# Seven products of 2x2 block sums for 6 of 16 row blocks in both MLPs, weights in groups of three blocks

## The chip, the cores and the metric

The kernel runs on one core of one Trainium2 chip. The metric is device time in microseconds of one execution; the median of 3 runs of the kernel before is 2336.47 us (2336.16 to 2338.05). The engines of the core are named as the profile names them: PE (TensorE, matrix products), PEld (its weight loads), DVE (VectorE), ACT (ScalarE), POOL (GpSimd), SP (SyncE, which issues the loads of the weights).

## The reference, cut to what matters

A two-layer encoder for 256 tokens of width 2048, all in float32: a sparse-attention mixer in layer 0, a convolution module in layer 1, and behind each of them an MLP of hidden width 8192 and a gated embedding. The change is in the two MLPs.

```python
D_MODEL, SEQ, D_FF = 2048, 256, 8192

def sq_relu_mlp(hn, w1, w2):
    a = jax.nn.relu(hn @ w1)
    return (a * a) @ w2

def reference(...):
    h = x
    for i in range(2):
        hn = rmsnorm(h, norm_mix_g[i])
        h = h + (dsa_mixer(hn, ...) if i == 0 else conformer_conv(hn, ...))
        h = h + sq_relu_mlp(rmsnorm(h, norm_mlp_g[i]), mlp_w1[i], mlp_w2[i])
        h = h + jax.nn.sigmoid(h @ ple_w_gate[i]) * (p[i] @ ple_w_proj[i])
    return rmsnorm(h, final_g)
```

## The kernel before, in words

Every large product is `gemm(x, src)` (L205): 256 tokens (two tiles `t` of 128) by 2048 rows of weights (16 row blocks `k` of 128) by 512 columns. The two token tiles accumulate in two PSUM banks `pm[0]`, `pm[1]`. For float32 accuracy each operand is a pair of parts of 12 significant bits, high and low, and one block product is three matmuls (L189 to L191): high by high, high by low, low by high. The activations stand as pairs `xh`, `xl` (128 features on the partitions, 16 blocks, 256 tokens). The weights are loaded by SP as they are, four row blocks to a transfer of 1 MB (`KG` = 4, tile `raw`, 4 buffers), and split in the kernel two blocks at a time: ACT copies `raw` to the high part `wh` (L181), DVE subtracts to get the low part `wl` (L185); 5 buffers each. PE then does 12 matmuls with these two blocks: 2 blocks, 2 token tiles, 3 parts.

An MLP (L568) goes over its hidden width in four parts of 2048 (`blk`). In a part, four gemms with columns of `w1` give the hidden values; `act` applies relu and the norm's factor (ACT, L579), squares (DVE, L580), and one step later PE transposes (L587, 4 of 128x128 for each token tile) and `split` (L212, ACT L215 and DVE L216) makes the pair `a`. Then four gemms with rows of `w2` follow, and DVE adds their banks to the residual stream `h` (`add_h`, L276). An MLP is so 32 gemms of 96 matmuls, and both together 64.

Work that belongs to a finished product (evictions, transposes) is put off into the following product by `defer` and `step` (L100, L103): a step is made for every two row blocks. The order on each engine is set by a scheduler that takes the recorded instructions with a priority by their place in the program and its own estimate of when their operands and buffers are ready. The profile's times are the chip's, not this estimate's. Each engine then works through its own list in order; a waiting instruction holds up all behind it.

In the convolution module some of the subtractions run on POOL. The first products of the kernel wait for the first transfers; the last gemm (L627) does the products of token tile 1 from the 6th row block on last, so that the end of tile 0 lies beside them.

Of the kernel before, what the change touches and what calls it, by code (L numbers as in the profile page):

```python
# [23 lines left out]
KG = 4  # L24
# [27 lines left out]
POOL_FROM = 1  # L52


@with_exitstack
def encoder(ctx: ExitStack, tc: tile.TileContext, A, inv_freq, out):
# [31 lines left out]
    def work(*shape):  # L88
        """A tile of up to 512 words per partition, from one rotation."""
        return shaped(small.tile([P, NB], F32, name="work", tag="work", bufs=6), shape)  # L90

    def held(*shape):
        """The same, from the rotation of tiles that live longer."""
        return shaped(small.tile([P, NB], F32, name="held", tag="held", bufs=5), shape)

# [61 lines left out]

    def blocks(w, n0, n=NB):
        return w.rearrange("(k p) n -> p k n", p=P)[:, :, n0:n0 + n]

    def gemm_part(pm, x, src, k0, kn, kt, low=None, dma=KG, apart=99):
# [3 lines left out]
        raw, rest = None, []  # L165
        for j in range(0, kn, 2):
            step()
            k = k0 + j
            if j % dma == 0:
                d = min(dma, kn - j)  # L170
                raw = wpool.tile([P, KG, NB], F32, name="raw", tag="raw", bufs=4)[:, :d, :n]
                if len(src.shape) == 3:
                    nc.sync.dma_start(raw, src[:, k:k + d])
                else:
                    m = src.shape[3]
                    for s in range(src.shape[2]):
                        nc.sync.dma_start(raw[:, :, s * m:(s + 1) * m], src[:, k:k + d, s])
            r = raw[:, j % dma:j % dma + 2, :]
            wh = wpool.tile([P, 2, NB], F32R, name="wh", tag="wh", bufs=5)[:, :, :n]
            wl = wpool.tile([P, 2, NB], F32R, name="wl", tag="wl", bufs=5)[:, :, :n]  # L180
            recent[0] = nc.scalar.activation(wh, r, AF.Copy).ins  # L181
            eng = low or nc.vector
            if callable(eng):
                eng = eng(k)
            eng.tensor_tensor(wl, r, wh.bitcast(F32), op=ALU.subtract)  # L185
# [7 lines left out]
            if j >= apart:  # L193
                for i in range(2):
                    products(i, 0)
                    rest.append(lambda i=i, products=products: products(i, 1))
            else:
                order = [(i, t) for i in range(2) for t in range(TT)]
                if k + 2 == kt:
                    order.sort(key=lambda v: v[1])  # L200
                for i, t in order:
                    products(i, t)
        return rest

    def gemm(x, src, low=None, tiles=mm_tile, dma=KG):  # L205
        step()
        pm = [tiles() for _ in range(TT)]
        kt = src.shape[1]
        gemm_part(pm, x, src, 0, kt, kt, low, dma)
# [11 lines left out]
    def rpow(dst, src, eps, scale=1.0):  # L221
        """dst = (scale * src + eps) ** -0.5"""
# [5 lines left out]
    class Norm:  # L228
        """Sums of squares of h by chunk, and in the end 1 / rms of every token."""
# [23 lines left out]

    def h_half(kk, x, g):
# [4 lines left out]
        if g is None:  # L259
            split(x[0][:, kk:kk + 2, :], x[1][:, kk:kk + 2, :], pt.rearrange("p k t f -> p k (t f)"))  # L260
        else:
            for k in range(2):
                split(x[0][:, kk + k, :], x[1][:, kk + k, :], pt[:, k].rearrange("p t f -> p (t f)"),
                      g[:, kk + k:kk + k + 1])
# [18 lines left out]
    def embedding(i):  # L283
        """The per-layer embedding, transposed and split."""
# [5 lines left out]
        ph = small.tile([P, 2, S], F32R, name="ph", bufs=1)  # L290
        pl = small.tile([P, 2, S], F32R, name="pl", bufs=1)
# [25 lines left out]
    # =================== layer 0: sparse attention ===================  # L317
    with tc.tile_pool(name="att", bufs=1) as att:
# [16 lines left out]
        def angles():  # L335
            """cos and sin of the rotary angles"""
# [24 lines left out]
        def rope(v, t, nh, rot):  # L361
            """v [P, nh, 128]: rotate the first `rot` of each head, in place"""
# [11 lines left out]
        def heads(pm, rot, dst):  # L374
            """[tokens, heads x 128] in PSUM -> scaled, rotated, transposed to dst [P, heads, S]"""
# [16 lines left out]
        norm0 = norm  # L392
        vv = att.tile([P, TT, NB], F32, name="vv")
        pm = gemm(xA, blocks(w_in, V0), dma=2)
# [153 lines left out]
        pms = []  # L548
        for c in range(2):
            step()  # L550
            pms.append([mm_tile() for _ in range(TT)])
            gemm_part(pms[c], xB, w_out[:, :, c * NB:(c + 1) * NB], 0, KT - KG, KT)
        flush()

    xA = xpair("A")
    norm = Norm()
    for c in range(4):
        w = w_out[:, :, c * NB:(c + 1) * NB]
        if c < 2:
            pm = pms[c]  # L560
            gemm_part(pm, xB, w, KT - KG, KG, KT)
        else:
            pm = gemm(xB, w)
        defer(0, lambda c=c, pm=pm: add_h(c, pm))
        h_chunk(c, xA, gcol["mlp0"], norm)

    # =================== squared-ReLU MLP ===================
    def mlp(layer, x, norm, other, xname):  # L568
        w1, w2 = A["mlp_w1"][layer], A["mlp_w2"][layer]
        xn = None  # L570
        for blk in range(4):
            a = xpair(other)

            def act(c, pm, a):
                rs = []
                for t in range(TT):
                    r = held(4, P)
                    rf = r.rearrange("p k f -> p (k f)")
                    nc.scalar.activation(rf, pm[t], AF.Relu, scale=norm[t])  # L579
                    nc.vector.tensor_tensor(rf, rf, rf, op=ALU.mult)  # L580
                    rs.append(r)

                def turn():
                    for t in range(TT):
                        pt = tr_tile().rearrange("p (k f) -> p k f", k=4)
                        for k in range(4):
                            nc.tensor.transpose(pt[:, k, :], rs[t][:, k, :], ident)  # L587
                        sl = (slice(None), slice(4 * c, 4 * c + 4), slice(t * P, (t + 1) * P))
                        split(a[0][sl], a[1][sl], pt)
                defer(1, turn)  # L590

            for c in range(4):
# [4 lines left out]
            for c in range(4):  # L597
                pm = gemm(a, blocks(w2[blk * D:(blk + 1) * D], c * NB))
                defer(0, lambda c=c, pm=pm: add_h(c, pm))
                if blk == 3:  # L600
                    h_chunk(c, xn)
        return xn

    # =================== gated per-layer embedding ===================
# [59 lines left out]
    xA = mlp(0, xA, norm, "B", "A")  # L664
# [5 lines left out]
    # =================== layer 1: convolution module ===================  # L670
    with tc.tile_pool(name="cnv", bufs=1) as cnv:
# [31 lines left out]
        def conv_pe(kk):  # L703
            """Depthwise convolution as products with diagonal matrices."""
# [18 lines left out]
        def conv_dve(tiles):  # L723
            """Depthwise convolution of one or two tiles, in two independent chains of sums."""
# [114 lines left out]
        xB = xpair("B")  # L839
        norm = Norm()  # L840
        for c in range(4):
            bb = cnv.tile([P, NB], F32, name="bb", tag="bb", bufs=2)
# [9 lines left out]
    xB = mlp(1, xB, norm, "A", "B")  # L852
# [55 lines left out]
```

## Time and profile before

| | us |
|---|---|
| median of 3 runs | 2336.47 |
| span of the profiled execution, first to last instruction | 2334.4 |
| PE busy | 2317.6 |
| PEld busy | 1928.5 |
| DVE busy | 1381.5 |
| ACT busy | 1109.4 |
| POOL busy | 243.0 |

The span is that of the profiled execution; the time of that execution around its span is not shown, so that the difference to the median, 2.07 us, stands for what lies outside. "Busy" adds up the recorded intervals of an engine, overlaps counted once. For PE they are modelled ends of pipelined matmuls: two matmuls that follow each other overlap in the record, and the distance of their starts says what one takes of PE's time.

### The profile page before, as it was taken

To read this page: it belongs to the slowest core of one execution; us is meant where nothing else is said; L and a number is where in the kernel's file an instruction comes from. 1 tells how busy PE (TensorE), PEld (TensorE's weight loads), DVE (VectorE), ACT (ScalarE), POOL (GpSimd) and SP (SyncE) were. 2 spreads that over 40 slices of the span, in tenths; PEclk is the share of its full clock that TensorE was granted. 3 is DMA by queue.
4 is the path that set the end of the run, shared out by engine and by line. 5 is a ranking of instruction groups with operands and counts; after the bars stand their busy time and mean duration, and the time that the engine had idled before them with its cause. 6 is when DMAs were issued, how large, how long until landed. Compare 5 with 4: busy or idle time off the path is not lost.

```text
span 2334.4 us, 27458 instructions
## 1 busy us (share of the span) xinstructions
PE 2317.6 (99%) x10798; PEld 1928.5 (83%) x10798; DVE 1381.5 (59%) x1796; ACT 1109.4 (48%) x1424; POOL 243.0 (10%) x169
## 2 busy tenths in 40 slices
PE   9999999999999999999999999999999999999998
PEld 7888888888888888888898887888888888888886
DVE  5658655555555554555658997555555555455555
ACT  6555555444444443444554745444344344344454
POOL 0112200000000000000049861000000000000001
PEclk9999999999999999999999999999999999999999
DMA  7544456556555556555646543555555555555553
GB/s 259 198 163 162 145 164 196 173 188 198 181 193 190 187 187 198 180 188 168 212 145 216 181 145 126 187 185 192 190 188 183 196 187 192 192 187 183 180 195 109
DMA packets 241378, 425.52 MB, mean 182 GB/s; under 512 B 8148, under 2 KB 54116, under 8 KB 241120
## 3 DMA queue, kind: packets, MB, share of 16 engines
q1 hardware_dynamic: 238384, 419.61, 55.3%
q10 hardware_dynamic: 2864, 4.15, 0.6%
q8 instruction: 85, 1.39, 0.2%
q14 instruction: 45, 0.37, 0.0%
HBM read 421.63 MB, written 2.10 MB: 182 GB/s over the span
## 4 chain that ended last, share of the span: by engine, by line
PE 98%; DVE 0%; issue 0%; DMA 0%; ACT 0%; SPq 0%; POOL 0%; POOLq 0%; DVEq 0%
PE pm L189 31%; PE pm L190 31%; PE pm L191 31%; PE pt L587 1%; PE pm L711 1%; PE pt L258 1%; PE at L497 0%; PE at L450 0%; PE at L527 0%; DMA raw<-in_a_w_in 0%; PE pt L387 0%; PE at L189 0%; PE at L190 0%; PE at L191 0%; PE pt L782 0%
## 5 line engine op out<-in xcount | busy, mean ns | idle before, releaser
L185 DVE TENSOR_TENSOR wl<-raw,wh 128x1024 fp32r<-128x1024 f32 (+1 forms) x739 | 903.6, 1223 | 805.1 <-ACT wh L181 804.2
L181 ACT ACTIVATE wh<-raw 128x1024 fp32r<-128x1024 f32 (+1 forms) x816 | 845.2, 1036 | 986.6 <-PE pm L191 968.7
L189 PE MATMUL pm<-wh,xhA 128*128 128x512 f32 (+2 forms) x1632 | 635.1, 390 | 0.4 <-ACT wh L181 0.3
L190 PE MATMUL pm<-wl,xhA 128*128 128x512 f32 (+2 forms) x1632 | 634.5, 389 | 0.0
L191 PE MATMUL pm<-wh,xlA 128*128 128x512 f32 (+2 forms) x1632 | 630.3, 388 | 0.8 <-DVE xlA L831 0.8
L189 PE MATMUL pm<-wh,xhB 128*128 128x512 f32 (+1 forms) x1600 | 612.2, 384 | 0.0
L190 PE MATMUL pm<-wl,xhB 128*128 128x512 f32 (+1 forms) x1600 | 611.8, 383 | 0.0
L191 PE MATMUL pm<-wh,xlB 128*128 128x512 f32 (+1 forms) x1600 | 610.9, 382 | 0.0
L189 PEld LDWEIGHTS pm<-wh,xhA 128*128 128x128 f32 x1632 | 306.7, 188 | 62.0 <-ACT wh L181 0.7
L191 PEld LDWEIGHTS pm<-wh,xlA 128*128 128x128 f32 x1632 | 306.4, 188 | 61.8 <-DVE xlA L831 1.7
L190 PEld LDWEIGHTS pm<-wl,xhA 128*128 128x128 f32 x1632 | 306.7, 188 | 60.9 <-DVE wl L185 0.8
L191 PEld LDWEIGHTS pm<-wh,xlB 128*128 128x128 f32 x1600 | 300.8, 188 | 56.9 <-issue 0.2
L189 PEld LDWEIGHTS pm<-wh,xhB 128*128 128x128 f32 x1600 | 300.8, 188 | 56.7 <-issue 0.2
L190 PEld LDWEIGHTS pm<-wl,xhB 128*128 128x128 f32 x1600 | 300.9, 188 | 56.7 <-issue 0.2
L740 DVE SCALAR_TENSOR_TENSOR at<-u,wdw,at 128x256 f32<-128x256 f32 x402 | 160.3, 481 | 0.0
L185 POOL TENSOR_TENSOR wl<-raw,wh 128x1024 fp32r<-128x1024 f32 (+1 forms) x77 | 157.2, 2058 | 27.7 <-ACT wh L181 27.0
L846 POOL TENSOR_TENSOR h<-bb,h 128x512 f32<-128x512 f32 x8 | 10.2, 1296 | 794.8 <-issue 794.8
L864 POOL TENSOR_TENSOR h<-h,gb 128x512 f32<-128x512 f32 x6 | 9.9, 1642 | 783.3 <-ACT work L237 783.3
L579 ACT ACTIVATE held<-pm,rstd 128x512 f32<-128x512 f32 x64 | 44.0, 687 | 31.0 <-PE pm L191 31.0
L580 DVE TENSOR_TENSOR held<-held 128x512 f32<-128x512 f32 x64 | 44.1, 688 | 16.2 <-ACT held L579 16.0
L276 DVE TENSOR_TENSOR h<-pm,h 128x512 f32<-128x512 f32 x80 | 51.4, 681 | 2.9 <-PE pm L191 2.9
L215 ACT ACTIVATE xhA<-pt 128x512 fp32r<-128x512 f32 x40 | 23.9, 597 | 31.0 <-PE pt L587 22.7
(156 smaller groups left out, 924.0 us busy)
## 6 DMA issues: line engine op xcount, KB each, us to landing
raw<-in_mlp_w SPq DMA_DIRECT2D x256, 1024.0 KB, 5.1
raw<-in_a_w_in SPq DMA_DIRECT2D x32, 1024.0 KB, 5.0
raw<-in_ple_w_gate SPq DMA_DIRECT2D x32, 1024.0 KB, 5.1
raw<-in_b_w_pw SPq DMA_DIRECT2D x48, 512.0 KB, 4.6
raw<-in_a_w_out SPq DMA_DIRECT2D x16, 1024.0 KB, 5.1
raw<-in_b_w_pw SPq DMA_DIRECT2D x16, 1024.0 KB, 5.1
raw<-in_b_w_pw SPq DMA_DIRECT2D x32, 256.0 KB, 3.1
raw<-in_a_w_in SPq DMA_DIRECT2D x12, 512.0 KB, 3.6
```

Of the source, the lines that this page charges most:

```text
L181: recent[0] = nc.scalar.activation(wh, r, AF.Copy).ins
L185: eng.tensor_tensor(wl, r, wh.bitcast(F32), op=ALU.subtract)
L189: nc.tensor.matmul(pm[t][:, :n], a, wh[:, i], start=k + i == 0, stop=False)
L190: nc.tensor.matmul(pm[t][:, :n], a, wl[:, i], start=False, stop=False)
L191: nc.tensor.matmul(pm[t][:, :n], b, wh[:, i], start=False, stop=k + i == kt - 1)
L215: nc.scalar.activation(dh, src, AF.Copy)
L258: nc.tensor.transpose(pt[:, k, t, :], h[:, t, (kk + k) * P:(kk + k + 1) * P], ident)
L276: nc.vector.tensor_tensor(hs, pm[t], hs, op=ALU.add)
L579: nc.scalar.activation(rf, pm[t], AF.Relu, scale=norm[t])
L580: nc.vector.tensor_tensor(rf, rf, rf, op=ALU.mult)
L587: nc.tensor.transpose(pt[:, k, :], rs[t][:, k, :], ident)
L740: nc.vector.scalar_tensor_tensor(dst, src, w, z, op0=ALU.mult, op1=ALU.add)
```

## The change

The 16 row blocks of a product in the MLPs are cut in two: blocks 0 to 5 and blocks 6 to 15. Two neighbouring column groups of 512 are now done together (`pair_gemm`), in four banks `y` (token tile 0, first columns), `z` (tile 0, second), `v` (tile 1, first), `x` (tile 1, second). Blocks 6 to 15 are done as before (`plain`). Blocks 0 to 5 are taken as three 2x2 problems: two token tiles by an even and an odd row block by two column groups. In place of eight block products there are seven (`seven`), each of a sum of activation blocks by a sum of weight blocks; a product serves for more than one output, so that banks are read in the middle of their accumulation: `x` three times and `z` once.

The weights of the seven products are four transfers of three row blocks each: `a` (even blocks, first columns), `b` (even, second), `c` (odd, first), `d` (odd, second). DVE makes the sums of weights in place, four additions of 128x1536 a pair: a+b, then +d, then +c in `a`, and b+d in `b`. Each of the seven is then split like any weight. The sums of activations are made when the activations are transposed (`Sums.put`): for each of three pairs of blocks two copies by ACT, five DVE operations of 128x128, and a split of 4 and of 3 blocks.

In the first product of an MLP the four readings of unfinished banks are copies by ACT (L726); the finished bank is combined with them by DVE (L731), and relu and square are both ACT's (L732, L733). In the second product all eight readings are DVE additions into `h` (L760).

All weights, in the other products too, are loaded and split in groups of two or three blocks (`KG` = 3; 16 blocks are 2, 3, 3, 2, 3, 3) with 6 buffers for `raw` and 4 for `wh` and `wl`. Three smaller things move with it: `held` has 8 buffers, the bias `bb` lies in `work`, and the depthwise taps are fetched during the output projection.

```diff
-KG = 4
+KG = 3
...
+SP = 3
+HELD = 8
+RAWS = 6
+SPLITS = 4
...
+    class Sums:
...
+        def put(self, kk, pt, g=None):
+            if kk >= 2 * SP:
+                h, l = (v[:, kk - 2 * SP:kk - 2 * SP + 2, :] for v in self.rest)
+                put_blocks((h, l), pt, None if g is None else g[:, kk:kk + 2])
+                return
+            y, z, v = work(4, P), work(4, P), work(2, P)
+            for k, dst in ((0, v), (1, z[:, 1:3, :])):
+                nc.scalar.activation(dst, pt[:, k], AF.Copy, scale=g[:, kk + k:kk + k + 1] if g is not None else 1.0)
+            x11, x21, x12, x22 = v[:, 0, :], v[:, 1, :], z[:, 1, :], z[:, 2, :]
+            tt = nc.vector.tensor_tensor
+            nc.vector.tensor_scalar(y[:, 0, :], x11, -1.0, None, op0=ALU.mult)
+            tt(y[:, 2, :], x21, x11, op=ALU.subtract)
+            tt(y[:, 3, :], x21, x22, op=ALU.subtract)
+            tt(y[:, 1, :], x11, y[:, 3, :], op=ALU.subtract)
+            tt(z[:, 0, :], x12, y[:, 1, :], op=ALU.subtract)
+            i = kk // 2
+            for dst, src in ((self.four, y), (self.more, z[:, :3, :])):
+                split(dst[0][:, :, i, :], dst[1][:, :, i, :], src)
...
+    def pair_gemm(x, src, taken, first=False):
+        bank = {"x": at_tile(), "y": mm_tile(), "v": mm_tile(), "z": mm_tile()}
...
+        def product(v, a, b, w, last=False):
+            for j, (l, r) in enumerate(((a, w[0]), (a, w[1]), (b, w[0]))):
+                left[v] -= 1
+                nc.tensor.matmul(bank[v], l, r, start=v not in begun, stop=bool(left[v] == 0 or (last and j == 2)),
+                                 skip_group_check=v in again)
...
+        def add(name, other):
+            nc.vector.tensor_tensor(raw(name), raw(name), raw(other), op=ALU.add)
...
+        def seven(m, v, name, plus=None, part=None):
+            step()
+            if plus:
+                raw(name), raw(plus)
+                add(name, plus)
+            w = halves(raw(name))
+            for i in range(SP):
+                product(v, x.sums(0, m, i), x.sums(1, m, i), (w[0][:, i], w[1][:, i]), part is not None and i == SP - 1)
+            if part:
+                defer(0, lambda: taken(part, bank[v]))
...
+        ks = groups(2 * SP, KT - 2 * SP)
+        raw("a")
+        seven(0, "x", "a", part="x1")
+        seven(5, "y", "c")
+        plain(0, ks[0])
+        seven(3, "z", "a", "b", part="z1")
+        plain(0, ks[1])
+        raw("d")
+        seven(1, "x", "a", "d", part="x2")
+        for r in ks[2:]:
+            plain(0, r)
+        seven(4, "z", "d")
+        seven(2, "x", "b", "d", part="x3")
+        plain_n2 = list(ks)
+        seven(6, "v", "a", "c")
+        for r in plain_n2:
+            plain(1, r)
...
+    def halves(r, low=None):
+        wh, wl = (wpool.tile([P, KG, NB], F32R, name=v, tag=v, bufs=SPLITS)[:, :r.shape[1], :r.shape[2]] for v in ("wh", "wl"))
+        recent[0] = nc.scalar.activation(wh, r, AF.Copy).ins
+        (low or nc.vector).tensor_tensor(wl, r, wh.bitcast(F32), op=ALU.subtract)
+        return wh, wl
...
-            for c in range(4):
-                pm = gemm(x, blocks(w1, blk * D + c * NB))
-                defer(0, lambda c=c, pm=pm, a=a: act(c, pm, a))
+                def taken(what, bank):
+                    if what in early:
+                        rs[early[what]] = held(4, P)
+                        nc.scalar.activation(rs[early[what]].rearrange("p k f -> p (k f)"), bank, AF.Copy)
+                        return
+                    t, n = where[what]
+                    r = rs[what]
                     rf = r.rearrange("p k f -> p (k f)")
+                    nc.vector.tensor_tensor(rf, bank, rf, op=ALU.subtract if what in minus else ALU.add)
+                    nc.scalar.activation(rf, rf, AF.Relu, scale=norm[t])
+                    nc.scalar.activation(rf, rf, AF.Square)
...
+            for ch in range(2):
+                pair_gemm(x, blocks(w1, blk * D + ch * 2 * NB, 2 * NB), hidden(ch, a))
...
-                pm = gemm(a, blocks(w2[blk * D:(blk + 1) * D], c * NB))
-                defer(0, lambda c=c, pm=pm: add_h(c, pm))
+                    hs = h[:, t, c * NB:(c + 1) * NB]
+                    less = what in early and early[what] in minus
+                    nc.vector.tensor_tensor(hs, hs, bank, op=ALU.subtract if less else ALU.add)
...
+            for ch in range(2):
+                pair_gemm(a, blocks(w2[blk * D:(blk + 1) * D], ch * 2 * NB, 2 * NB), residual(ch, blk == 3))
```

How this stands on the engines is shown at three places. The first is DVE in the second products of an MLP (rows with `w2`). Before, eight splits of weights (`wl`) and two additions of banks to `h` make one gemm:

```order
L185 TENSOR_TENSOR wl<-raw,wh 128x1024 x6
L276 TENSOR_TENSOR h<-pm,h 128x512 x2
L185 TENSOR_TENSOR wl<-raw,wh 128x1024 x8
L276 TENSOR_TENSOR h<-pm,h 128x512 x2
L185 TENSOR_TENSOR wl<-raw,wh 128x1024 x8
L276 TENSOR_TENSOR h<-pm,h 128x512 x2
```

In the changed kernel the splits are of two or three blocks, and sums of weights (`raw<-raw`) and readings of unfinished and finished banks stand between them:

```order
L299 TENSOR_TENSOR wl<-raw,wh 128x1536
L246 TENSOR_TENSOR raw<-raw 128x1536
L760 TENSOR_TENSOR h<-h,pm 128x512
L299 TENSOR_TENSOR wl<-raw,wh 128x1536
L299 TENSOR_TENSOR wl<-raw,wh 128x1024
L246 TENSOR_TENSOR raw<-raw 128x1536
L299 TENSOR_TENSOR wl<-raw,wh 128x1536 x2
L760 TENSOR_TENSOR h<-h,at 128x512
L299 TENSOR_TENSOR wl<-raw,wh 128x1536 x2
L760 TENSOR_TENSOR h<-h,pm 128x512
```

What moved: a reading of a bank stands once or twice between two splits, so that a split can stand behind an instruction that waits for PE.

The second place is DVE at the start of the second pair of a `w1` part, where the hidden values of the first pair become operands. Before, the transposed values (`pt`) are split by one operation for each token tile between splits of weights:

```order
L185 TENSOR_TENSOR wl<-raw,wh 128x1024 x6
L580 TENSOR_TENSOR held<-held 128x512 x2
L185 TENSOR_TENSOR wl<-raw,wh 128x1024 x2
L216 TENSOR_TENSOR xlB<-pt,xhB 128x4x128 x2
L185 TENSOR_TENSOR wl<-raw,wh 128x1024 x6
```

In the changed kernel the sums of activations (`work<-work`, two puts side by side) and their splits stand there:

```order
L246 TENSOR_TENSOR raw<-raw 128x1536
L193 TENSOR_SCALAR work<-work 128x128
L194 TENSOR_TENSOR work<-work 128x128
L195 TENSOR_TENSOR work<-work 128x128
L193 TENSOR_SCALAR work<-work 128x128
L194 TENSOR_TENSOR work<-work 128x128
L195 TENSOR_TENSOR work<-work 128x128
L299 TENSOR_TENSOR wl<-raw,wh 128x1024
L731 TENSOR_TENSOR held<-pm,held 128x512
L196 TENSOR_TENSOR work<-work 128x128 x2
L731 TENSOR_TENSOR held<-at,held 128x512
L197 TENSOR_TENSOR work<-work 128x128 x2
```

What moved: 16 operations of DVE come in one cluster (two puts of five, two combinations of banks, and the four splits of the puts behind them) where four stood before.

The third place is PE in a pair with `w2`. Before, the products of a row block stand in turn for both token tiles (banks `pm_4761` and `pm_4762`), the three parts of one weight together:

```order
L189 MATMUL pm_4761<-wh_4829,xhA_2774 128x512
L190 MATMUL pm_4761<-wl_4830,xhA_2774 128x512
L191 MATMUL pm_4761<-wh_4829,xlA_2775 128x512
L189 MATMUL pm_4762<-wh_4829,xhA_2774 128x512
L190 MATMUL pm_4762<-wl_4830,xhA_2774 128x512
L191 MATMUL pm_4762<-wh_4829,xlA_2775 128x512
```

In the changed kernel the product of a+b into bank `z` (`pm_6705`, weights `wh_6759` and `wl_6760`) is begun with its high part, and two products with the high part of the next weights (`wh_6775`) are put ahead of its low part:

```order
L230 MATMUL pm_6705<-wh_6759,xhB_5733 128x512
L230 MATMUL pm_6703<-wh_6775,xhB_5733 128x512
L230 MATMUL pm_6704<-wh_6775,xhB_5733 128x512
L230 MATMUL pm_6705<-wl_6760,xhB_5733 128x512
L230 MATMUL pm_6705<-wh_6759,xlB_5735 128x512
L230 MATMUL pm_6705<-wh_6759,xhB_5733 128x512
L230 MATMUL pm_6705<-wl_6760,xhB_5733 128x512
```

What moved: high parts are used one group earlier than the order of the program says; no matmul is added by it. Over the whole program the rows of PE count 10,662 matmuls before and 10,374 in the changed kernel.

## Rows read from the trace of the kernel before

**Rows 1.** The page: busy us (share of the span) and instructions of each engine.
```profile
PE 2317.6 (99%) x10798; PEld 1928.5 (83%) x10798; DVE 1381.5 (59%) x1796; ACT 1109.4 (48%) x1424; POOL 243.0 (10%) x169
```
**Rows 2.** The page: the chain that ended last, by engine.
```profile
PE 98%; DVE 0%; issue 0%; DMA 0%; ACT 0%; SPq 0%; POOL 0%; POOLq 0%; DVEq 0%
```
**Rows 3.** Waits of PE: who waited for whom, us in total, times, longest.
```profile
PE pt L258 <- DVE xlA L219: 1.5, 1, 1.5
PE pm L191 <- DVE xlA L831: 0.8, 2, 0.4
...
PE pm L189 <- ACT wh L181: 0.3, 1, 0.3
```
**Rows 4.** Stretches: two w1 gemms, two w2 gemms, part of an MLP, the start.
```profile
core 0: us, PE busy (x) PEld busy (x) DVE busy (x) ACT busy (x) POOL busy (x), PEclk, DMA share, GB/s
743.60:788.90 45.30, 45.30 (x210) 37.58 (x209) 24.93 (x24) 21.60 (x25) 0.00 (x0) 1.00 0.59 193
840.00:883.50 43.50, 43.50 (x194) 36.02 (x193) 22.01 (x20) 16.96 (x17) 0.00 (x0) 1.00 0.60 193
700.00:1000.00 300.00, 300.00 (x1353) 248.69 (x1352) 158.16 (x148) 130.80 (x137) 0.00 (x0) 1.00 0.59 189
12.00:40.00 28.00, 27.86 (x128) 22.61 (x129) 21.86 (x39) 21.73 (x40) 1.72 (x1) 1.00 0.94 328
```
**Rows 5.** Timeline of PE in a w2 gemm: start us, us, engine, line, operation.
```profile
480.27 0.39 PE L189 MATMUL pm<-wh,xhB 128*128 128x512 f32 x1
480.50 0.39 PE L190 MATMUL pm<-wl,xhB 128*128 128x512 f32 x1
480.72 0.39 PE L191 MATMUL pm<-wh,xlB 128*128 128x512 f32 x1
480.95 0.39 PE L189 MATMUL pm<-wh,xhB 128*128 128x512 f32 x1
```
**Rows 6.** The chain in order of time: four transposes, and the matmul behind them.
```profile
1961.81 0.44 PE pt L587 x4
1962.24 0.23 PE pm L189
```
**Rows 7.** Groups by line and shape: count, busy us, mean ns, idle before.
```profile
L185 DVE TENSOR_TENSOR wl<-raw,wh 128x1024 fp32r<-128x1024 f32 x715 | 884.0, 1237 | 783.7 <-ACT wh L181 782.9 <-issue 0.3
L185 DVE TENSOR_TENSOR wl<-raw,wh 128x512 fp32r<-128x512 f32 x16 | 11.3, 707 | 14.3 <-ACT wh L181 14.1
L276 DVE TENSOR_TENSOR h<-pm,h 128x512 f32<-128x512 f32 x80 | 51.4, 681 | 2.9 <-PE pm L191 2.9
L216 DVE TENSOR_TENSOR xlB<-pt,xhB 128x512 fp32r<-128x512 f32 x40 | 27.3, 691 | 16.5 <-ACT xhB L215 16.5
L427 DVE TENSOR_TENSOR ki<-ki,kg 128x128 f32<-128x128 f32 x2 | 0.6, 288 | 0.0
L343 DVE TENSOR_SCALAR work<-work 128x128 f32<-128x128 f32 x1 | 0.2, 221 | 0.0
L181 ACT ACTIVATE wh<-raw 128x1024 fp32r<-128x1024 f32 x768 | 813.0, 1059 | 938.6 <-PE pm L191 921.6 <-issue 10.1 <-DMA raw<-in_a_w_in 2.1
L181 ACT ACTIVATE wh<-raw 128x512 fp32r<-128x512 f32 x40 | 25.2, 631 | 37.4 <-PE pm L191 36.5 <-ACT wh L181 0.7
L579 ACT ACTIVATE held<-pm,rstd 128x512 f32<-128x512 f32 x64 | 44.0, 687 | 31.0 <-PE pm L191 31.0
```
**Rows 8.** Timeline of DVE: a split and two additions without idle time between.
```profile
733.44 1.23 DVE L185 TENSOR_TENSOR wl<-raw,wh 128x1024 fp32r<-128x1024 f32 x1 [1.49 <-ACT wh L181]
734.59 1.28 DVE L276 TENSOR_TENSOR h<-pm,h 128x512 f32<-128x512 f32 x2
```
**Rows 9.** Transfers: issues, KB each, median us from issue to landing.
```profile
raw<-in_mlp_w SPq DMA_DIRECT2D x256, 1024.0 KB, 5.1
raw<-in_a_w_in SPq DMA_DIRECT2D x12, 512.0 KB, 3.6
```
**Rows 10.** Timeline of ACT at the start.
```profile
14.95 1.06 ACT L181 ACTIVATE wh<-raw 128x1024 fp32r<-128x1024 f32 x1 [0.35 <-DMA raw<-in_a_w_in]
```

More of the change, by code (lines that the diff above doesn't have):

```diff
@@ L158, in blocks, with put_blocks, load, raw @@
+    def put_blocks(x, pt, g):
+        if g is None:
+            split(x[0], x[1], pt.rearrange("p k t f -> p k (t f)"))
+        else:
+            for k in range(2):
+                split(x[0][:, k, :], x[1][:, k, :], pt[:, k].rearrange("p t f -> p (t f)"), g[:, k:k + 1])
     def blocks(w, n0, n=NB):
         return w.rearrange("(k p) n -> p k n", p=P)[:, :, n0:n0 + n]
-    def gemm_part(pm, x, src, k0, kn, kt, low=None, dma=KG, apart=99):
+    def pair_gemm(x, src, taken, first=False):
+        bank = {"x": at_tile(), "y": mm_tile(), "v": mm_tile(), "z": mm_tile()}
+        begun, again, left = set(), set(), {"x": 3 * SP, "y": SP, "v": SP, "z": 2 * SP}
+        for v in left:
+            left[v] += KT - 2 * SP
+            left[v] *= 3
+        def load(ks, n):
+            raw = raw_tile(len(ks))
+            nc.sync.dma_start(raw, src[:, ks.start:ks.stop:ks.step, n * NB:(n + 1) * NB])
+            return raw
+        def product(v, a, b, w, last=False):
[3 more added lines that the diff above has]
+                                 skip_group_check=v in again)
+                begun.add(v)
+            if left[v] == 0:
+                defer(0, lambda: taken(v, bank[v]))
+            elif last:
+                again.add(v)
+        raws = {}
+        def raw(name):
+            if name not in raws:
+                raws[name] = load(range(name in "cd", 2 * SP, 2), int(name in "bd"))
+            return raws[name]
+        def add(name, other):
[10 more added lines that the diff above has]
+                defer(0, lambda: taken(part, bank[v]))
+        def plain(n, ks):
+            step()
+            w = halves(load(ks, n))
+            for t, v in enumerate("zx" if n else "yv"):
+                if t == 1 and len(ks) > 2:
+                    step()
+                for i, k in enumerate(ks):
+                    product(v, x.block(0, k, t), x.block(1, k, t), (w[0][:, i], w[1][:, i]))
+        ks = groups(2 * SP, KT - 2 * SP)
[15 more added lines that the diff above has]
+            plain(1, r)
@@ new lines, in groups, with raw_tile @@
+    def groups(k0, kn):
+        n = -(-kn // KG)
+        ends = [k0 + kn * i // n for i in range(n + 1)]
+        return [range(i, j) for i, j in zip(ends, ends[1:])]
+    def raw_tile(nk, n=NB):
+        return wpool.tile([P, KG, NB], F32, name="raw", tag="raw", bufs=RAWS)[:, :nk, :n]
+    def halves(r, low=None):
[3 more added lines that the diff above has]
+        return wh, wl
@@ L163, in gemm_part @@
+    def gemm_part(pm, x, src, k0, kn, kt, low=None, apart=99):
         xh, xl = x
         n = math.prod(src.shape[2:])
[L165 to L185, printed above, removed]
+        rest = []
+        for ks in groups(k0, kn):
+            k = ks.start
+            if (k - k0) % 2 == 0:
+                step()
+            raw = raw_tile(len(ks), n)
+            if len(src.shape) == 3:
+                nc.sync.dma_start(raw, src[:, k:k + len(ks)])
+            else:
+                m = src.shape[3]
+                for s in range(src.shape[2]):
+                    nc.sync.dma_start(raw[:, :, s * m:(s + 1) * m], src[:, k:k + len(ks), s])
+            wh, wl = halves(raw, low(k) if callable(low) else low)
@@ L568, in mlp, with out_projection @@
-    def mlp(layer, x, norm, other, xname):
+    def out_projection(pool):
+        x = Sums("A", pool)
+        norm = Norm()
+        for c in range(4):
+            w = w_out[:, :, c * NB:(c + 1) * NB]
+            if c < 2:
+                pm = pms[c]
+                gemm_part(pm, xB, w, KT - 4, 4, KT)
+            else:
+                pm = gemm(xB, w)
+            defer(0, lambda c=c, pm=pm: add_h(c, pm))
+            h_chunk(c, x, gcol["mlp0"], norm)
+        return x, norm
+    def mlp(layer, x, norm, other, xname, pool):
@@ L569, in mlp @@
         w1, w2 = A["mlp_w1"][layer], A["mlp_w2"][layer]
         xn = None
+        where = {"y": (0, 0), "z": (0, 1), "v": (1, 0), "x": (1, 1)}
+        early = {"x1": "y", "x2": "z", "x3": "v", "z1": "x"}
+        minus = ("y", "v")
         for blk in range(4):
[L572 to L577, printed above, removed]
-                    rf = r.rearrange("p k f -> p (k f)")
[L579 to L590, printed above, removed]
```

111 lines of the change are left out of this document (72 added, 39 removed).

## The prediction, made before the changed kernel ran

> **What bounds the kernel now.** The page's busy times come first: PE 99%, DVE 59%, ACT 48% [rows 1]. The chain that ended last says whether that busy engine sets the end: 98% of it is PE, no other engine reaches 1% [rows 2]. Third, PE's own waits: nine rows, 7.1 us together, all at the start, around the convolution's norm, none in an MLP [rows 3]. So PE is never kept waiting by the splits. Fourth, the stretches of the MLPs: there PE is busy all the time at full clock, while DVE works 24.9 of 45.3 us for two w1 gemms and 22.0 of 43.5 us for two w2 gemms [rows 4]. Each high part waits for PE to free a buffer (921.6 us over the run) and each low part for the high one [rows 7]: ACT and DVE are throttled by PE, not the other way round.
>
> What one matmul costs is read from the distance of starts, 480.27 to 480.95 for three, 0.2267 us [rows 5], not from its recorded 0.39 us, which overlaps the next. 192 of them make 43.5 us, and that is the whole w2 stretch. A w1 pair has 16 transposes more, four in 0.44 us [rows 6], 1.8 us in all.
>
> The Trainium skill (Perfetto Trace Analysis, Identifying the Most-Contended Engine) warns that matmul busy time is a bad measure of distance from the limit and asks for the busy share of weight loads. That share is 83% here [rows 1]; by it PE would have room and removing matmuls might free less than their spacing. I come back to that as a rival.
>
> **The change part by part.**
>
> Removed from PE: a pair of column groups had 16 x 2 x 2 x 3 = 192 matmuls. Now seven products of 3 blocks and 3 parts are 63, and 10 plain blocks are 120, together 183. There are 32 pairs, so 288 fewer; the order shows the same, 10,662 to 10,374. At 0.2267 us that is 65.3 us. Nothing is added to PE, the transposes are as many as before. With 183 a pair takes 41.5 us (w2) or 43.2 us (w1).
>
> Added to DVE: this decides whether the 65.3 us arrive. The prices: a split of 1024 columns takes 1.24 us, of 512 takes 0.71 [rows 7], so 512 more columns cost 0.53, and an operation of 1536, which the trace does not have, 1.77 by duration. Back to back, operations overlap: the addition after a split begins 1.15 us after it, and of two additions that take 1.28 together the second takes 0.68, so the first holds DVE for 0.60 [rows 8], some 0.08 less than the durations. That gives the lower price.
> - Splits: 11 of 1536 and 4 of 1024, 24.4 us; four sums of weights, 7.1 us. Together 31.5 us a pair.
> - w2: eight additions into h at 0.68 [rows 7], 5.4 us. Sum 36.9 us by duration, 34.7 with 27 operations at 0.08 less, of 41.5 us.
> - w1: four combinations, 2.7; plain puts, 2.5 a pair at 0.69, 1.7; 1.5 sum puts, each 0.22 and four at 0.29 for 128 columns, 0.69 and about 0.57 for the splits, 2.6 together [rows 7], 4.0. Sum 39.9 us by duration, 37.0 by spacing (36 operations), of 43.2 us.
>
> So DVE goes from 51 to 55% to 84 to 92% of a pair, and stays below PE. ACT: 11 x 1.49 and 4 x 1.06 for the high parts, 20.6 us; twelve copies, relus and squares at 0.69, 8.2 us; puts under 6 us: at most 35 of 43.2 us in w1.
>
> Shares are not enough, since a late split stops PE at once. How far DVE runs ahead: with four buffers the high part of a group may be begun when PE has finished the group four back, so three groups lie between. A seven takes PE 2.04 us, a plain group 2.72 or 4.08. The shortest three are d, b+d, a+c: 6.1 us, ahead of a plain group of two, whose split needs 1.06 + 1.24 us; otherwise 6.8 us or more against 1.49 + 1.77. At least 3.5 us of margin is left: about two more operations of 1.77 may stand in front of a split. In the w2 pairs one sum and one addition stand there, sometimes behind a wait for a bank; I take 0 for them. The tightest is bank x, read after its third product and written again 3.4 us later, with two splits in front of the reading; bounds 0 to 1 us a pair, nearest the stretches in which such readings of banks cost PE nothing [rows 4].
>
> The cluster: in the second w1 pair of each part, DVE has from the split of a to that of a+b+d eight operations of 1.77, one of 1.24, two combinations and two sum puts: 22.1 us, or 20.2 by spacing. PE gives it 9.4 us before the pair starts and 13.8 us in it (with 8 transposes), 23.2. It fits with 1 to 3 us to spare if DVE never idles, but the plain group before is due 4 us earlier and can come up to 1.9 us late. Bounds 0 and 1.9 us for eight such pairs, 0 to 15 us; the spacing is the nearer row, so I take 0.5 us each, 4 us.
>
> Transfers: as many bytes as before, in pieces of 512 and 768 KB. The share of the DMA engines is 0.59 and would be 0.62. Landing takes 3.6 us for 512 KB, 5.1 for 1 MB [rows 9], so 768 KB about 4.4. Four of six raw buffers hold a to d; the other two are refilled when their split is done, about three groups before PE reaches it. I take 0 and treat the rest as a rival.
>
> The start: DMA is busy 0.94 of the time from 12 to 40 us [rows 4], and ACT waited 0.35 us for the third transfer [rows 10]. The second is now 768 KB: 0.8 us later at 328 GB/s, its split up to 1.0 us longer. Bounds 0 and 1.8 us; I take 1 us.
>
> Elsewhere groups of three do the same columns in fewer operations, and PE does not wait there [rows 3]; 0, within 2 us either way. The end of the last gemm has 24 instead of 30 matmuls (5.4 instead of 6.8 us) over the end of token tile 0, whose chain behind the same kind of operations needs about 4 us: 0.
>
> **Sum.** 2334.4 - 65.3 + 4 + 1 = 2274.1 us span. The median lies 2.07 us above the span of before, so 2276 us.
>
> **Rivals.**
> - DVE's queue makes PE wait in every pair. For it: 92% of a pair by duration, readings of banks that wait for PE in front of splits, and the order on PE, which takes high parts of the next weights ahead of missing low parts. Against it: the margin of 3.5 us and the overlap [rows 8]. At 1 us in each of 32 pairs: 2336.5 - 65.3 + 32 = 2303 us.
> - PE's spacing is not its own limit. The skill (TensorE: Matmul & The Clock Gate, Back-to-back issue gap) gives about 131 ns for sustained matmuls of 512 columns; the 227 ns here speak against that price. As a mechanism: something beside PE paces the matmuls, and a removed one gives back only part of its spacing. At 131 ns, which is the page's figure and an estimate, 288 give 37.7 us, 2299 us. From rows alone: if half of the spacing came back, 2304 us. Against it: no wait is recorded, and every start is 0.2267 apart.
> - Slower: the weights come late. a, b, c and d hold four of six raw buffers for most of a pair, so each plain load waits for a split and the split for the load. If one landing of 4.4 us a pair is left open to PE, a pair loses 4.4 and gains 2.04: 32 x 2.4 = 75 us more, 2412 us. It decides from 2.04 us a pair on, 4.7% of it. Against it: a plain load has about 6 us between its buffer and its need.
> - That the matmuls do not go away is excluded by the count of the order.
>
> **How the numbers follow.** Forecast 0.66 (its own range 2268 to 2286), DVE's queue 0.21, PE's pace 0.03, late weights 0.06, other losses 0.04. The range 2268 to 2308 leaves out the far end of DVE's queue and the late weights; below, it takes the full 65.3 us and 3 us from elsewhere. About 0.2%, 4.7 us, is what a measurement can tell from no change. Faster needs less than 1.9 us lost in a pair: all of the forecast, PE's pace, and most of DVE's queue, 0.88; same 0.04; slower 0.08.
>
> **What would show it.** 288 matmuls fewer (10,510 on the page), starts 0.2267 us apart; DVE about 1860 us busy (16 x 15.0 and 16 x 14.9 us more), near 85% in w2 and 90% in w1 pairs; PE waits for DVE's low parts under 10 us in total, most in the second w1 pairs; w2 pairs of 41.5 and w1 pairs of 43.2 to 44 us. The forecast is wrong if PE waits for low parts in every pair, if the high parts wait for transfers, or if operations of 1536 columns take well over 1.8 us.

## Result, and the profile after

The changed kernel takes 2275.53 us (median of 4 runs, 2273.53 to 2276.31), the kernel before 2337.18 in the same comparison: a ratio of 0.9733, 95% interval 0.9719 to 0.9747. It is faster, by 61.7 us; 2276 us had been forecast, for the reason that the experiments below bear out. A second series gave 2274.51 and 0.9732 (0.9718 to 0.9745).

The page of the changed kernel, its span, the busy times and the chain by engine, beside [rows 1, 2]:

```profile
span 2271.8 us, 27693 instructions
...
PE 2253.1 (99%) x10510; PEld 1873.6 (82%) x10510; DVE 1783.6 (79%) x2075; ACT 1298.4 (57%) x1530; POOL 248.5 (11%) x150
...
PE 98%; ACT 0%; DMA 0%; issue 0%; DVE 0%; POOL 0%; SPq 0%; POOLq 0%; DVEq 0%; ACTq 0%
```

PE has 288 instructions and 64.5 us less, DVE 402 us more, and yet PE alone is still the chain. The span is 62.6 us shorter than the 2334.4 of before. What DVE's time is made of, by line and shape (beside [rows 7]):

```profile
L299 DVE TENSOR_TENSOR wl<-raw,wh 128x1536 fp32r<-128x1536 f32 x450 | 789.7, 1765 | 243.4 <-ACT wh L298 241.9
L299 DVE TENSOR_TENSOR wl<-raw,wh 128x1024 fp32r<-128x1024 f32 x184 | 229.0, 1245 | 92.2 <-ACT wh L298 91.2
L246 DVE TENSOR_TENSOR raw<-raw 128x1536 f32<-128x1536 f32 x128 | 224.6, 1754 | 19.0 <-DMA raw<-in_mlp_w 18.0
```

An operation of 1536 columns takes 1.765 or 1.754 us; the 1.77 made from two smaller shapes holds. The three stretches are a second w1 pair, the first and the second w2 pair of a part, in the columns of [rows 4], but of two gemms each, from first matmul to first matmul:

```profile
592.37:635.76 43.39, 43.39 (x201) 35.97 (x199) 38.05 (x41) 31.55 (x38) 0.00 (x0) 1.00 0.61 194
635.76:678.16 42.40, 42.40 (x192) 35.18 (x191) 36.20 (x31) 23.91 (x21) 0.00 (x0) 1.00 0.61 199
508.43:549.91 41.48, 41.48 (x184) 34.36 (x183) 34.89 (x28) 20.55 (x15) 0.00 (x0) 1.00 0.60 203
```

PE is busy for the whole of each. 183 matmuls at 0.2267 us are 41.48, and the last stretch is 41.48; the second has 8 transposes more, the first 16. The waits of PE (us in all, times, longest) are again nine, as in [rows 3], and none is in an MLP; the first, the fourth and the last row of the list:

```profile
PE pt L404 <- issue: 1.5, 1, 1.5
...
PE pt L923 <- DVE stats L924: 1.0, 2, 0.5
...
PE pm L323 <- ACT xhB L355: 0.4, 1, 0.4
```

The transfers (count, KB, median us to landing) and who waited for them, beside [rows 9]:

```profile
raw<-in_mlp_w SPq DMA_DIRECT2D x256, 768.0 KB, 6.1
raw<-in_mlp_w SPq DMA_DIRECT2D x128, 512.0 KB, 4.5
```
```profile
ACT wh L298 <- DMA raw<-in_mlp_w: 32.2, 24, 2.8
...
DVE raw L246 <- DMA raw<-in_mlp_w: 18.0, 10, 2.6
```

Landing takes 6.1 us, not the 4.4 that I worked out. The size alone is not the reason, since pieces of 768 KB land in 4.5 us in E1 below, which has the same groups; what makes them late in the pairs was not tried. ACT and DVE do wait for weights, PE does not.

### The profile page after: what moved, and what is told of

The parts are those of the page before. It is cut to its first block, busy times and chain, and to the rows that moved or that the text cites. A ratio compares the mean times of both kernels' runs of the same rounds, so it can differ in the third digit from the quotient of the medians.

```text
span 2271.8 us, 27693 instructions
## 1 busy us (share of the span) xinstructions
PE 2253.1 (99%) x10510; PEld 1873.6 (82%) x10510; DVE 1783.6 (79%) x2075; ACT 1298.4 (57%) x1530; POOL 248.5 (11%) x150
## 4 chain that ended last, share of the span: by engine, by line
PE 98%; ACT 0%; DMA 0%; issue 0%; DVE 0%; POOL 0%; SPq 0%; POOLq 0%; DVEq 0%; ACTq 0%
PE pm L230 40%; PE at L230 18%; PE pm L323 11%; PE pm L325 11%; PE pm L324 11%; PE pt L745 1%; PE pm L880 1%; PE pt L404 1%; PE at L591 0%; PE at L638 0%; PE at L668 0%; DMA raw<-in_a_w_in 0%; PE pt L528 0%; PE at L323 0%; PE at L324 0%
## 5 line engine op out<-in xcount | busy, mean ns | idle before, releaser
L298 ACT ACTIVATE wh<-raw 128x1536 fp32r<-128x1536 f32 (+4 forms) x710 | 942.8, 1335 | 757.5 <-PE at L230 255.4
L299 DVE TENSOR_TENSOR wl<-raw,wh 128x1536 fp32r<-128x1536 f32 (+2 forms) x652 | 1033.7, 1598 | 356.8 <-ACT wh L298 354.2
L246 DVE TENSOR_TENSOR raw<-raw 128x1536 f32<-128x1536 f32 x128 | 224.6, 1754 | 19.0 <-DMA raw<-in_mlp_w 18.0
L323 PE MATMUL pm<-wh,xhA 128*128 128x512 f32 (+2 forms) x608 | 234.1, 388 | 1.4 <-ACT xhA L999 1.2
L324 PE MATMUL pm<-wl,xhA 128*128 128x512 f32 (+2 forms) x608 | 233.8, 385 | 0.0
L325 PE MATMUL pm<-wh,xlA 128*128 128x512 f32 (+2 forms) x608 | 231.8, 385 | 0.5 <-DVE xlA L1000 0.4
L324 PE MATMUL pm<-wl,xhB 128*128 128x512 f32 (+1 forms) x576 | 212.4, 369 | 0.0
L325 PE MATMUL pm<-wh,xlB 128*128 128x512 f32 (+1 forms) x576 | 211.5, 368 | 0.0
L323 PE MATMUL pm<-wh,xhB 128*128 128x512 f32 (+1 forms) x576 | 210.7, 369 | 0.4 <-ACT xhB L355 0.4
L230 PE MATMUL pm<-wl,xhB 128*128 128x512 f32 x528 | 206.6, 391 | 0.0
```

The costliest lines, as they stand in the source:

```text
L230: nc.tensor.matmul(bank[v], l, r, start=v not in begun, stop=bool(left[v] == 0 or (last and j == 2)), skip_group_check=v in again)
L246: nc.vector.tensor_tensor(raw(name), raw(name), raw(other), op=ALU.add)
L299: (low or nc.vector).tensor_tensor(wl, r, wh.bitcast(F32), op=ALU.subtract)
L323: nc.tensor.matmul(pm[t][:, :n], a, wh[:, i], start=k + i == 0, stop=False)
L324: nc.tensor.matmul(pm[t][:, :n], a, wl[:, i], start=False, stop=False)
L325: nc.tensor.matmul(pm[t][:, :n], b, wh[:, i], start=False, stop=k + i == kt - 1)
```

## The experiments

Theory: PE sets the pace, each matmul removed gives 0.2267 us, and DVE keeps ahead. The main rivals: DVE's queue is nearly late, or the weights are. Three runs take the edit apart, five more its margins; then comes a version with more of it.

**E1, the groups alone.** Both MLPs with eight products, the groups of two and three blocks and the three smaller things kept.

```diff
-        x = Sums("A", pool)
+        x = xpair("A")
...
-            for ch in range(2):
-                pair_gemm(x, blocks(w1, blk * D + ch * 2 * NB, 2 * NB), hidden(ch, a))
+            for c in range(4):
+                pm = gemm(x, blocks(w1, blk * D + c * NB))
+                defer(0, lambda c=c, pm=pm, a=a: act(c, pm, a))
```

> The MLPs are done with eight block products as before (192 matmuls a pair, 10,798 on the page); groups of two or three row blocks, the buffers and all else stay as in the changed kernel. Theory (the gain is the 288 matmuls at 0.2267 us, the rest of the change moves 2 to 3 us): 2337 to 2341 us, no matmul of the MLPs waits. Rival (the groups of three and their buffers carry a part of the gain): under 2332 us. Rival (they cost and the seven products earn more than their count): over 2345 us.

2338.94 us against 2338.28, ratio 1.0006 (0.9996 to 1.0015). The groups are worth nothing that can be measured, so that the whole gain is that of the seven products. Its busy times:

```profile
PE 2318.0 (99%) x10798; PEld 1927.2 (82%) x10798; DVE 1348.3 (58%) x1613; ACT 1076.5 (46%) x1222; POOL 245.5 (11%) x150
```

From the first matmul of the first MLP to the last matmul of the kernel E1 takes 2327.40 - 379.72 = 1947.68 us and the changed kernel 2261.49 - 379.10 = 1882.39: 65.29 us less, where 288 x 0.2267 is 65.3.

**E2, four of 16 blocks.** `SP` is here a constant of the kernel, the number of pairs of row blocks that go through seven products, and not the engine.

```diff
-SP = 3
+SP = 2
```

> Only row blocks 0 to 3 go through seven products; a pair has 42 + 144 = 186 matmuls, 192 fewer than before in all. Theory (each matmul that goes is worth its spacing of 0.2267 us, whatever DVE has to do): 43.5 us less than before, and the 2 to 3 us of the groups more: 2294 to 2297 us. Rival (something beside PE paces it, a removed matmul gives back less; here DVE has some 5 us a pair less to do than with six blocks): the gain is not in proportion to the count, 2302 us or more, or already near 2276 us because DVE was what held the six-block version back.

2296.38 us, ratio 0.9825 (0.9809 to 0.9841). 192 matmuls fewer than E1 (10,606 on the page), 42.6 us less by the medians and 43.0 by the spans, and 192 x 0.2267 = 43.5. The price of a matmul holds at a second size.

**E3, no sums of weights.** The four additions of weights in a pair are left out.

```diff
             if plus:
                 raw(name), raw(plus)
-                add(name, plus)
+                pass
```

> The four sums of weights of a pair are left out, so the products use the unsummed weights; PE, ACT and the transfers have the same work, DVE 225 us less. Theory (all of DVE's added work is covered): the same time as the changed kernel, 2274 to 2278 us. Rival (late low parts are where 2.7 us of the 65.3 went, or more is hidden in PE's sequence): 2270 to 2273 us.

2275.50 us, ratio 0.9734 (0.9720 to 0.9749), with DVE 196 us less busy (1587.4). The same time: the four sums, about half of the 402 us that the change adds to DVE, are hidden in full. For the rest it is the absence of waits of PE that says so.

**E4, four low parts twice.** DVE repeats the low parts of the four sum groups in each pair: 4 x 1.67 = 6.7 us more.

```diff
-            w = halves(raw(name))
+            w = halves(raw(name), again=1 if plus else 0)
...
-        (low or nc.vector).tensor_tensor(wl, r, wh.bitcast(F32), op=ALU.subtract)
+        for _ in range(1 + again):
+            (low or nc.vector).tensor_tensor(wl, r, wh.bitcast(F32), op=ALU.subtract)
```

> The low parts of the four summed weights are computed twice, 4 x 1.68 = 6.7 us more for DVE in a pair; DVE was idle 6.6 us of a w2 pair and 5.3 to 7.2 us of a w1 pair. Theory (the idle time can be used almost whole; DVE binds only when it is used up): 2280 to 2310 us, with PE waiting for low parts mostly in the second w1 pairs. Rival (the idle time of DVE is waiting that other work can't fill, since a split stands behind an operation that waits for PE): most of the 6.7 us shows in each of 32 pairs, 2400 us or more.

2376.58 us, ratio 1.017 (1.0155 to 1.0185): 101 us over the changed kernel, 3.2 a pair, between the two. The same three stretches, and the three largest waits of PE:

```profile
606.52:654.02 47.50, 44.21 (x201) 35.80 (x199) 45.88 (x50) 31.79 (x38) 0.00 (x0) 1.00 0.53 177
654.02:697.98 43.96, 42.69 (x192) 35.10 (x191) 42.14 (x35) 23.79 (x21) 0.00 (x0) 1.00 0.57 192
517.18:562.38 45.20, 42.07 (x184) 34.20 (x183) 41.68 (x32) 20.31 (x15) 0.00 (x0) 1.00 0.55 186
```
```profile
PE pm L230 <- DVE wl L300: 34.8, 29, 2.9
PE at L230 <- DVE wl L300: 26.5, 21, 1.7
PE pt L746 <- ACT held L734: 15.7, 10, 2.0
```

DVE had 6.6 us idle in the third stretch and could not use them: given 6.8 us more work, the pair grows by 3.7. The third wait is that of the transposes for the hidden values of ACT, so not all of the loss is at the low parts.

**E5, two low parts twice.** Only those of a+b and b+d, 3.35 us a pair, which is less than the margin of 3.5 us in the prediction. The repeat in `halves` is that of E4.

```diff
-            w = halves(raw(name))
+            w = halves(raw(name), again=1 if part in ("z1", "x3") else 0)
...
```

> The low parts of a+b and b+d alone are computed twice, 3.35 us more for DVE in a pair. With four repeated, 6.7 us, a pair came out 3.2 us longer on the mean, so 3.5 us could be filled. Theory (a margin of some 3.5 us a pair, then loss one for one): 2275 to 2290 us. Rival (the loss grows from the first added operation on, in proportion: half of what is added shows): 1.6 us in 32 pairs, 2320 to 2330 us.

2312.76 us, ratio 0.9891 (0.9876 to 0.9906): 37 us lost, 1.2 a pair, again between the two. Here the reason can be read. The group a+b+d of the second w2 pair, in the changed kernel (pair begins at 508.43) on DVE, ACT and PE, and in E5 (510.87); start and duration in us, and in brackets the idle time before and who ended it:

```profile
514.61 1.75 DVE L246 TENSOR_TENSOR raw<-raw 128x1536 f32<-128x1536 f32 x1
517.92 0.69 DVE L760 TENSOR_TENSOR h<-h,pm 128x512 f32<-128x512 f32 x1 [1.56 <-PE pm L230]
518.53 2.89 DVE L299 TENSOR_TENSOR wl<-raw,wh 128x1536 fp32r<-128x1536 f32 x2
...
516.48 2.44 ACT L298 ACTIVATE wh<-raw 128x1536 fp32r<-128x1536 f32 x2 [3.99 <-DVE raw L246]
...
522.03 0.39 PE L230 MATMUL at<-wl,xhB 128*128 128x512 f32 x1
```
```profile
520.19 1.76 DVE L246 TENSOR_TENSOR raw<-raw 128x1536 f32<-128x1536 f32 x1
523.59 1.76 DVE L300 TENSOR_TENSOR wl<-raw,wh 128x1536 fp32r<-128x1536 f32 x1 [1.64 <-ACT wh L298]
...
522.07 5.19 ACT L298 ACTIVATE wh<-raw 128x1536 fp32r<-128x1536 f32 x4 [7.41 <-DVE raw L246]
...
525.40 0.50 PE L230 MATMUL at<-wl,xhB 128*128 128x512 f32 x1
```

A sum group is a chain of three: the sum, then the high part, then the low part, and each waits for the one before. In the changed kernel the sum begins 6.18 us into the pair, the low part ends at 520.28 (the first of the two in that row; the recorded time of one is 1.75), and PE takes it at 522.03: 1.75 us to spare. An addition to `h` that waits for PE (at 517.92) stands in front of the low part too. In E5 the two repeated low parts in front (one is that of b+d of the pair before) put the sum at 9.32 us, and the low part ends at 525.35; PE takes it at 525.40, so that nothing is left. By then PE is already 0.93 us late in the pair (14.53 us after its beginning, in place of 13.60). The same match for all 32 pairs, group by group in their order, leaves 0.1 us or less at a+b+d in 28 of them. PE's waits in E5:

```profile
PE at L230 <- DVE wl L300: 4.5, 5, 1.4
PE pm L230 <- ACT wh L298: 4.5, 10, 0.4
PE at L230 <- ACT wh L298: 3.6, 8, 0.5
```

They are 12.6 of the 37 us. A matmul's recorded end lies 0.16 us behind the next start, so that shorter waits leave no idle time in the record. By the distances of starts, about two thirds of the loss stand in front of matmuls that take a high part and one third in front of those that take a low part. The high parts are late with the sums: ACT waits 105.0 us for sums in E5, 52.9 us in the changed kernel, and in the rows above four high parts follow each other after such a wait (522.07).

**E6, three buffers for the parts.**

```diff
-SPLITS = 4
+SPLITS = 3
```

> Three buffers for high and low parts in place of four; all work is the same. A high part can be begun when the group three back is done, so two groups lie between, 4.1 us between sevens, against 3.3 us for the two parts of a split; under one operation of 1.76 us fits in front. Theory (the lead that the buffers allow, not DVE's share of busy time, is what covers DVE): PE waits in every pair, 2 to 6 us, 2340 to 2470 us. Rival (the share decides, DVE is idle 16% of a pair): under 2290 us.

2289.54 us, ratio 0.9793 (0.9777 to 0.9809): the lead theory falls, 14 us are lost, not over 60. A second w1 pair and a second w2 pair:

```profile
597.36:641.70 44.34, 43.83 (x201) 35.87 (x199) 39.67 (x45) 31.79 (x38) 0.00 (x0) 1.00 0.57 190
513.46:554.94 41.48, 41.48 (x185) 34.36 (x183) 34.88 (x28) 20.54 (x15) 0.00 (x0) 1.00 0.62 203
```

Only the second w1 pairs lose (0.94 us each, eight of them), and the last w2 pair of each MLP 0.3; the w2 pair shown loses nothing at all. So the fourth buffer is not what most of the margin hangs on. Another 4 us are lost ahead of the first MLP. The order on the engines moves with the buffers, and I cannot part the two.

**E7, five buffers for the weights as loaded.**

```diff
-RAWS = 6
+RAWS = 5
```

> Five buffers for raw weights in place of six; four hold a, b, c and d for most of a pair, so one is left for plain groups. Landing took 6.1 us in the changed kernel, and the split behind it 3.3 us. Theory (the sixth buffer is what keeps the transfers off PE's way): a plain group comes every 9 us where PE needs one every 4 to 6, 5 to 10 us lost a pair, 2430 to 2600 us. Rival (the transfers have much room): under 2285 us.

2409.53 us, ratio 1.0302 (1.0285 to 1.0319): 134 us lost, 4.2 a pair, less than the theory said, in its direction. PE's largest wait, and what ACT waited for:

```profile
PE pm L230 <- ACT wh L298: 69.1, 66, 2.8
...
ACT wh L298 <- DMA raw<-in_mlp_w: 185.0, 69, 6.2
```

The high parts wait 185.0 us for transfers, where the changed kernel has 32.2. This is the rival of the late weights, one buffer away.

**E8, plain blocks by two parts.** The third part (high by low activations) of the plain blocks is left out, 40 matmuls a pair, 9.1 us of PE.

```diff
-                    product(v, x.block(0, k, t), x.block(1, k, t), (w[0][:, i], w[1][:, i]))
+                    product(v, x.block(0, k, t), x.block(1, k, t), (w[0][:, i], w[1][:, i]), parts=2)
...
```

> In the plain blocks of the MLPs the third part of each product (low activations by high weights) is left out, 40 matmuls fewer a pair; ACT, DVE and the transfers have the same work. PE needs 143 x 0.2267 = 32.4 us and up to 1.9 us of transposes a pair, DVE works 34.9 to 38 us. Theory (DVE then binds, at about 93% busy): pairs of 37.5 to 39.6 us, 2110 to 2170 us. Rival (PE still binds, DVE's operations overlap further): 9.07 us less in 32 pairs, 1985 to 2000 us. Rival (waiting in DVE's list takes more as PE gets closer): over 2190 us.

2114.57 us, ratio 0.9041 (0.9028 to 0.9055): 161 us less where 1280 x 0.2267 = 290 us of PE's time are gone. A second w1 pair and a second w2 pair:

```profile
565.34:606.21 40.87, 37.32 (x161) 29.10 (x159) 40.15 (x47) 32.13 (x42) 0.00 (x0) 0.96 0.61 202
492.52:528.61 36.09, 33.92 (x145) 26.54 (x143) 34.13 (x28) 19.95 (x15) 0.00 (x0) 1.00 0.69 238
```

Now DVE is busy for 40.2 of 40.9 us and 34.1 of 36.1, close to its limit in these pairs, as the theory said. PE waits 26.1 us for low parts and 39.7 us for high parts of weights, and part of the time is a lower clock (0.96 in the first row). The two pairs are 2.5 and 5.4 us shorter than in the changed kernel, where PE needs all of the time.

**V0 and V1, the gate products of layer 0 as well.** V0 is the changed kernel again. V1 sends the gate products of the embedding of layer 0 through two more such pairs (18 matmuls fewer):

```diff
-    ple(0, xA, lambda c: h_chunk(c, xB, gcol["mix1"], norm1))
+        ple_pairs(0, xA, lambda c: h_chunk(c, xB, gcol["mix1"], norm1))
...
+            pair_gemm(x, blocks(A["ple_w_gate"][layer], ch * 2 * NB, 2 * NB), gated(ch, prs))
```

> The changed kernel itself, on the same chip as v1, as its yardstick: 2274 to 2277 us.

> In layer 0 the four gate products of the embedding also go through two pairs of seven products: 18 matmuls fewer, 10,492. Theory (PE sets the pace, DVE's queue has 2 to 4 us of room in a pair): 18 x 0.2267 = 4.1 us less than the changed kernel, about 2271.5 us, of which the sums of activations at the end of the MLP in front may take back up to 2 us. Rival (in these pairs DVE has 46 of 48.7 us to work, by the same prices, since each bank takes two operations more and the sums of activations lie in front; E5 lost time with 38 of 42.9): DVE is late and PE waits 2 us or more in each pair, 2276 us or more, no gain.

V0 2274.51 us (2273.80 to 2275.98), V1 2273.45 (2272.53 to 2275.29), ratio to before 0.9726 (0.9713 to 0.9739). The ranges overlap: 1.1 us by the medians, not 4.1, and not shown to be a gain. Two waits of PE are new in V1, both at the start of the new pairs:

```profile
PE pm L230 <- ACT wh L298: 1.2, 2, 0.9
...
PE pm L230 <- DVE wl L299: 0.6, 1, 0.6
```

These 1.8 us, and stretches between rows that no wait is recorded for, take back most of 4.1. No version that does all the products is shown to beat the changed kernel.

## Why the prediction was right, step by step

- **Removed, 65.3 us: right.** E1 and E2 measure 65.3 and 43.0 us for 288 and 192 matmuls. That refutes the rival of PE's pace, which would have left half of it. The Trainium skill (TensorE: Matmul & The Clock Gate, Back-to-back issue gap) gives about 131 ns for sustained matmuls of 512 columns; here a removed matmul gave back 227. The busy share of weight loads is 83% before, and 82% in the changed kernel and in E1, which has all the matmuls; PE was the limit in all three, so the share's distance from 100% was no room. The Trainium skill (Perfetto Trace Analysis, Identifying the Most-Contended Engine) asks for that share, and for the share of peak arithmetic, as the measure; for the share of weight loads this case's runs do not bear it out. The transposes are as many as I said, but 8 of the 16 that I put into each first w1 pair lie in the first w2 pair of the part, and both take some 42.4 us.
- **DVE's price, 36.9 or 34.7 us in w2 pairs and 39.9 or 37.0 in w1: the lower one, by spacing, was the better.** Two w2 pairs in turn have 36.2 and 34.9 us, two w1 pairs 35.2 and 38.1. DVE's busy total, 1783.6, is below the 1860 that I added up from durations, which count the overlaps twice.
- **DVE hidden: right, by less than I said.** The margin of "at least 3.5 us: about two more operations" is the step that failed without harm. I counted each split from the moment its buffer is free, a high and a low part, 1.49 + 1.77 us. But the sums are made in place: a+b+d can begin only when the low part of a+b has been made, and then sum, high part and low part follow one another, about 5 us. The trace has 1.75 us left at a+b+d in all eight second w2 pairs, and E5, with two operations more, loses 1.2 us a pair.
- **The rival of DVE's queue: absent in all 32 pairs, no wait of PE for a low part**, and none for the reading of bank x. E4, E5 and E8 show what it would be.
- **The cluster, 4 us: wrong, it is 0.** A second w1 pair takes 43.39 us, which is 183 matmuls and 16 transposes and nothing else. The fit by spacing (1 to 3 us to spare) was the right end; I had no row for the other. E6 shows how near it is: there these pairs are the first to lose. In the changed kernel the low part of the plain group of three behind a+b, the one that I had called due earlier, is ready 1.55 us before PE takes it in six of these eight pairs, 1.18 us in one, and 0.30 us in the pair of the first part of layer 1's MLP, where it ends at 1532.30:

```profile
1530.55 1.75 DVE L299 TENSOR_TENSOR wl<-raw,wh 128x1536 fp32r<-128x1536 f32 x1
...
1532.60 0.48 PE L230 MATMUL pm<-wl,xhB 128*128 128x512 f32 x1
```

- **Transfers, 0: right for PE, with a wrong landing (6.1 for 4.4 us).** "About 6 us between its buffer and its need" was then no margin, and ACT's 24 waits show it. With a buffer less (E7) the case is lost.
- **The start, 1 us: less than half.** The hundredth matmul of a product starts at 37.9 us, before at 37.5; in the second profile of the changed kernel at 37.8.
- **Elsewhere, 0 within 2: about 2.2 us lost.** With -65.3 and 0.4, this is what remains of the span's -62.6. Ahead of the first MLP 3.1 us are lost, with the 0.4 of the start. Some 2 us of them are the transposes of the taps, moved there from the first MLP and given back in it (717.02 us for that MLP before, 714.97 in E1). Some 0.5 us lie behind the last matmul. E1's median, 0.7 us above before, says that it is at the edge of what can be measured.

So the span came out 2.3 us under the 2274.1: the cluster 4 too high, the start 0.6 too high, the rest 2.2 too low. What I added for the time around the span, 2.07 us, compared a span with the median of other executions; of one execution it is 2273.53 - 2271.8 = 1.7. And the profiled execution is the shortest of the four; the spans of the others are 1.5 to 2.7 us longer. So it is in part luck that the forecast lies 0.5 us from the median, since errors of several us cancel; the 65.3 us are no luck.

## What to carry to other kernels

A matmul taken from the engine that is busy all the time is worth the distance of two starts, and an engine beside it may be filled to 84 to 88% if its instructions stand well ahead. Not the idle share tells how well, but the longest chain of operations that must follow one another before the consumer: here sum, high part, low part, with 1.75 us left of 6.6 us idle in a second w2 pair. The order of the list counts as well: in one second w1 pair a plain group had 0.30 us left. Ask of each pool of buffers what one less would cost, since the shares do not show which one is at its edge: here one of the six for loads is worth 134 us and one of the four for parts 14, with whatever the changed order of the engines adds to either.

## What the hardware showed that was not expected

In E7 a wait of PE costs more than the wait. PE in a w2 pair of it:

```profile
493.60 0.39 PE L230 MATMUL pm<-wh,xlB 128*128 128x512 f32 x1
496.81 1.22 PE L230 MATMUL pm<-wh,xhB 128*128 128x512 f32 x2 [2.83 <-ACT wh L298]
...
499.20 0.63 PE L230 MATMUL pm<-wh,xlB 128*128 128x512 f32 x1
499.63 0.63 PE L230 MATMUL pm<-wh,xhB 128*128 128x512 f32 x1
```
```profile
496.80:502.60 5.80, 5.64 (x12) 3.94 (x13) 5.25 (x4) 4.08 (x3) 0.00 (x0) 0.50 0.50 148
```

After 2.83 us without work the granted clock is at 0.50, the level of 1.2 GHz, for 5.8 us, and matmuls start 0.43 us apart in place of 0.23. E7's mean granted clock is 0.983, the changed kernel's 0.999; 0.016 of 2405.9 us is 38 us, an estimate, beside the 69 us of the waits themselves. Some 5 of the 38 lie at the start, where E7 has a granted clock of 0.50 from 8.0 to 18.2 us and the changed kernel 1.00; E1 has 0.67 there, so that this part is not due to these waits. In E4, with 77 us of waits in 60, the mean clock is 0.995; what tells the two apart was not tried. The clock was not in the price of the rival of the late weights.
